# A hybrid retention and delta-rule step: the first block's triangular inverse moved from VectorE and DMA to TensorE, and small scalings moved to ScalarE

## The chip, the cores and the metric

The kernel runs on one core of a Trainium2 chip. The metric is device time in microseconds from the start to the end of one execution; the time before is the median of three runs. A change of less than 0.3% can't be told from no change. TensorE is PE in the profile's rows, VectorE is DVE, ScalarE is ACT, GpSimd is POOL and SyncE is SP.

## The reference

One decoder layer for 2048 new tokens and for 8 short sequences of 8 tokens. Half of the heads are retention heads (`ret`), the other four are gated delta heads (`gdn`). For a delta head and a chunk of tokens the reference solves a unit lower triangular system and carries a state S:

```
kk = einsum('bhid,bhjd->bhij', ki, ki)
A = where(strict, bi[..., :, None] * kk * dmat, 0.0)
rhs = concatenate([ki * (bi * exp(cum))[..., None], vi * bi[..., None]])
sol = triangular_solve(eye + A, rhs, lower=True, unit_diagonal=True)
v_new = u - einsum('bhcd,bhde->bhce', w, S)
scores = einsum('bhid,bhjd->bhij', qi, ki) * dmat
o = einsum(qi * exp(cum), S) + einsum(scores, v_new)
S = exp(cum[-1]) * S + einsum(ki * tail, v_new)
```

q, k and v of a delta head pass through a causal convolution with four taps and a SiLU first. An output projection with two norms and an MLP (squared ReLU, width 4096) follow. All is float32; the large products are made from a high and a low part, three products for each.

## The kernel before, in words

The 2048 tokens are four blocks (b = 0 to 3) of T = 512, each of NC = 4 chunks of 128; the 64 short tokens ride with block 1. A block has three stages: the input projections of its heads (`proj`), the output projection (`out_proj`) and the MLP. The MLP of a block is merged with the projections of the next, so that from block 1 on the heads' small steps lie between large products of two kinds. Block 0 has no block before it: its heads have only its own projections beside them. Weights are split into high and low parts on their first use (ScalarE the high, GpSimd the low) and stored in memory for later blocks.

The order of TensorE's instructions is written out by the program: a planner (`Weave`) emits the main stream, and side streams (one or two heads at a time) give up the engine for a number of planned microseconds at each `yield LAT[...]`. In block 0 two delta streams run, heads 0 and 2 in one and 1 and 3 in the other. TensorE executes in this order, and an instruction whose data are late holds up all that are behind it. The tiles of heads 0 and 2 are called XX, ym, mt, kv; those of heads 1 and 3 lie in one page called bhi, and their q, k, v in blo.

`gdn_head` makes for a head: the decay matrix Dm (four operations, one for each chunk, which multiply by the upper mask U and by cc, the scale of k with beta), the products mt = (k k, k q) times Dm, then the inverse XT of the triangular matrix of each chunk, v scaled (vr), and the recurrence over the four chunks. The inverse is made in two parts. The blocks of 32 are inverted on VectorE, with moves of 16x16 blocks between partitions by 19 small DMAs for a head that GpSimd issues. Then two levels of doubling (32 and 64) on TensorE bring them to 128: transpose XT, copy it to X (ScalarE), multiply with the level's part ms of the matrix, copy to Y (ScalarE), multiply with XT, subtract from XT (VectorE).

```
px = v4(mx())
for c in range(NC):
    transpose(px[:, c], XT[:, c], P)
act(X, px, AF.Copy)
...
    matmul(py[:, c], ms[:, c], X[:, c])
act(Y, py, AF.Copy)
...
    matmul(pt[:, c], Y[:, c], XT[:, c])
tt(XT, XT, pt, ALU.subtract)
```

`conv_channel` makes the four taps of a convolution on VectorE: a product for the first tap, then three multiply-adds; there are 12 channels of 128 in each block. `act` is an operation of ScalarE, `tt`, `tsc` and `stt` are of VectorE (two tensors, tensor and scalars, two tensors and a scalar).

Of the kernel before, what the change touches and what calls it, by code (L numbers as in the profile page):

```python
# [21 lines left out]
H = 4  # L22
# [27 lines left out]
C_ER = C_VD + H  # L50
C_VDS = C_ER + H
C_ERS = C_VDS + H
C_END = C_ERS + H
C_L = C_END
C_LS = C_L + P
C_ALL = C_LS + NS
# [6 lines left out]
def const_table():  # L63
    i = np.arange(P)
    c = np.zeros((P, C_ALL), np.float64)
    c[:, C_ID:C_ID + P] = np.eye(P)
    c[:, C_U:C_U + P] = i[:, None] <= i[None, :]
    c[:, C_L:C_L + P] = i[:, None] > i[None, :]
    for n, s in enumerate(LEVELS):
        c[:, C_M + n * P:C_M + (n + 1) * P] = level_mask(i, s)  # L70
    same = i[:, None] // BB == i[None, :] // BB
    c[:, C_BD:C_BD + P] = same
    c[:, C_BS:C_BS + P] = -1.0 * (same & (i[:, None] < i[None, :]))
    j = np.arange(NS)
# [12 lines left out]
    return c.astype(np.float32)  # L87


def rope_table(nb):  # L90
# [8 lines left out]

TUNE = dict(  # L100
    first=dict(
        conv=7.29, inv=41.8, mem=7.63, pace=0.08, gate=10.83, h2=10.56, rstd=16.8, hk=1.57, put=1.7, gate2=1.82, sc=2.02, gs=9.72,
        g1=2.55, g2=2.75, g3=0.91, g4=2.06, g5=0.58, c1=1.61, c2=1.07, c3=0.99, glate=4.36, s1=7.06, s2=1.58, s3=0.83,
        s4=1.43, s5=0.98, s6=0.86, s7=1.7, r0=2.61, rs=1.89, r1=1.4, r2=2.98, r3=0.73, rlate=6.88, t1=7.35, t2=0.71,
        st=3.5, dg=1.65, n0=0.08, n1=2.49, n2=3.62, n3=1.1, f0=0.1, f1=1.8, f2=1.2),
# [97 lines left out]
def hybrid_kernel(ctx: ExitStack, tc: tile.TileContext, I, O, NB: int, SB: int):  # L203
# [48 lines left out]
    def stt(out, in0, scalar, in1, op0, op1):  # L252
        return V.scalar_tensor_tensor(out=out, in0=in0, scalar=scalar, in1=in1, op0=op0, op1=op1)  # L253

    def tt(out, a, b, op, eng=None):
        return (eng or V).tensor_tensor(out=out, in0=a, in1=b, op=op)  # L256

    def tsc(out, a, s1, s2, op0, op1=None, eng=None):
        if op1 is None:
            return (eng or V).tensor_scalar(out=out, in0=a, scalar1=s1, scalar2=None, op0=op0)  # L260
        return (eng or V).tensor_scalar(out=out, in0=a, scalar1=s1, scalar2=s2, op0=op0, op1=op1)
# [19 lines left out]
    Us = cst[:NS, C_US:C_US + NS]  # L281
    smask = [cst[:NS, C_MS + n * NS:C_MS + (n + 1) * NS] for n in range(len(SLEVELS))]
    bmask = cst[:NS, C_BM:C_BM + NSEQ]
    Lr = const.tile([P, P], F32R, name="Lr")
    Lsr = const.tile([NS, NS], F32R, name="Lsr")
    L, Ls = Lr.bitcast(F32), Lsr.bitcast(F32)
# [134 lines left out]
    class Block:  # L421
# [232 lines left out]
        def conv_channel(self, ct, pss, out, outs, raws):  # L654

            raw = page([P, NTM], "raw", bufs=2)
            V.tensor_copy(raw[:, 0:3], hist[:, ct, :])
            for (n0, n1), ps in zip(self.halves, pss):
                w = min(n1, T) - n0
                act(raw[:, 3 + n0:3 + n0 + w], ps[:, :w], AF.Copy)  # L660
                if n1 > T:
                    V.tensor_copy(raws[:, :, 3:], ps[:, T - n0:n1 - n0].rearrange("p (s l) -> p s l", s=NSEQ))
            V.tensor_copy(hist[:, ct, :], raw[:, T:T + 3])
            tsc(out, raw[:, 0:T], cw[:, ct, 0:1], None, ALU.mult)
            for j in range(1, 4):
                stt(out, raw[:, j:j + T], cw[:, ct, j:j + 1], out, ALU.mult, ALU.add)
            th = raw[:, 0:T]
            act(th, out, AF.Tanh)
            stt(out, th, 1.0, out, ALU.add, ALU.mult)
            if self.samp:  # L670
                V.tensor_copy(raws[:, :, 0:3], scv[:, ct])
                V.tensor_copy(scv[:, ct], raws[:, :, LS:LS + 3])
                y = outs.rearrange("p (s l) -> p s l", s=NSEQ)
                tsc(y, raws[:, :, 0:LS], cw[:, ct, 0:1], None, ALU.mult)
                for j in range(1, 4):
                    stt(y, raws[:, :, j:j + LS], cw[:, ct, j:j + 1], y, ALU.mult, ALU.add)
                th = junk()[:, :NS]
                act(th, outs, AF.Tanh)
                stt(outs, th, 1.0, outs, ALU.add, ALU.mult)
# [51 lines left out]
        def gdn_head(self, h):  # L731
# [48 lines left out]
            X, XT = XX[:, 0], XX[:, 1]  # L780
            Dm = X
            act(Dm.rearrange("p c i -> p (c i)"), ps, AF.Exp)
            for c in range(NC):
                stt(Dm[:, c], Dm[:, c], cc[:, c:c + 1], U, ALU.mult, ALU.mult)
            yield LAT["g1"]

            mt = get(mtp, "mt").rearrange("p (c a d) -> p c a d", c=NC, a=2)
            for cp in range(0, NC, 2):
                pm = mx().rearrange("p (c a i) -> p c a i", c=2, a=2)
                for c in (cp, cp + 1):  # L790
                    matmul(pm[:, c - cp], kq[:, 0, c * P:(c + 1) * P], kq[:, :, c * P:(c + 1) * P])
                tt(mt[:, cp:cp + 2], pm, Dm[:, cp:cp + 2].unsqueeze(2).to_broadcast([P, 2, 2, P]), ALU.mult)

            ym = quad(get(ymp, "ym"))
            Y, ms = ym[:, 0], ym[:, 1]
            nb = NC * NB16
            yf, prod = (ap.rearrange("p c d -> p (c d)") for ap in (Y, ms))
            w = NC * BB
# [53 lines left out]
            tt(XT.rearrange("p c (b i) -> p c b i", b=NB16), spread(xc), blk(bd), ALU.mult)  # L852
            tt(xo, spread(cm), blk(mask[0]), ALU.mult)
            tt(XT, XT, ms, ALU.subtract)

            pv = mx()
            for c in range(NC):
                transpose(pv[:, c * P:(c + 1) * P], vf[:, c * P:(c + 1) * P], P)
            tt(vr, v4(pv), per4(rin), ALU.mult)
            yield LAT["inv"]  # L860

            for n in range(1, len(LEVELS)):
                px = v4(mx())
                for c in range(NC):
                    transpose(px[:, c], XT[:, c], P)
                act(X, px, AF.Copy)
                tt(ms, mt[:, :, 0, :], bc4(mask[n]), ALU.mult, eng=G)
                yield LAT["g2" if n == 1 else "g5"]
                py = v4(mx())
                for c in range(NC):  # L870
                    matmul(py[:, c], ms[:, c], X[:, c])
                act(Y, py, AF.Copy)
                yield LAT["g3"]
                pt = v4(mx())
                for c in range(NC):
                    matmul(pt[:, c], Y[:, c], XT[:, c])
                tt(XT, XT, pt, ALU.subtract)
                yield LAT["g4"]
            W.signal(self.key(f"y{h}"))

            S = Sg[:, h, :]
            og = X
            so = small([P, 8], "so")
            for c in range(NC):
                kc, qc = kq[:, 0, c * P:(c + 1) * P], kq[:, 1, c * P:(c + 1) * P]
                p1 = mx()
                matmul(p1[:, :P], kc, S)
                matmul(p1[:, P:2 * P], qc, S)
                R = small([P, P], f"R{st}", bufs=1)
                stt(R, p1[:, :P], nce[:, c:c + 1], vr[:, c], ALU.mult, ALU.add)  # L890
                act(og[:, c], p1[:, P:2 * P], AF.Copy, scale=E[:, 0, h, c:c + 1])
                yield LAT["c1"]
                p2 = mx()
                matmul(p2[:, :P], XT[:, c], R)
                vn = small([P, P], f"vn{st}", bufs=1)
                act(vn, p2[:, :P], AF.Copy)
                yield LAT["c2"]
                p3 = mx()
                matmul(p3[:, P:2 * P], kt[:, c], vn)
                matmul(p3[:, :P], mt[:, c, 1, :], vn)  # L900
                stt(S, S, E[:, 2, h, c:c + 1], p3[:, P:2 * P], ALU.mult, ALU.add)
                tt(og[:, c], og[:, c], p3[:, :P], ALU.add)
                act(junk(), og[:, c], AF.Square, accum_out=so[:, c:c + 1])
                if c < NC - 1:
                    yield LAT["c3"]
            if b == NB - 1:
                nc.gpsimd.dma_start(O["gdn_p"][:, h, :], S)
            W.signal(self.key(f"q{h}"), 0.0)
            stt(so[:, :NC], so[:, :NC], 1.0 / DK, eq, ALU.mult, ALU.add)
            rsqrt(so[:, :NC], so[:, :NC], NC)  # L910
            tt(og, og, per4(so[:, :NC]), ALU.mult)
            yield LAT["glate"]
            po = mx()
            for c in range(NC):
                transpose(po[:, c * P:(c + 1) * P], og[:, c], P)
            self.put_mix(H + h, po, 0, zf)

        def gdn_sample(self, h):
            sc, LAT = self.sc, self.lat
# [624 lines left out]
```

## Time and profile before

| what | value |
|---|---|
| median of 3 runs | 3052.93 us (3044.34 to 3053.2) |
| the profiled execution | 3054.3 us, its span 3052.5 us |
| TensorE busy | 2857.7 us (94%) |
| VectorE busy | 1559.1 us (51%) |
| ScalarE busy | 879.6 us (29%) |
| GpSimd busy | 861.1 us (28%) |

The span is from the first to the last instruction. A busy TensorE is not one at its peak: its granted clock has two levels, and a matmul at the lower takes twice as long. What is idle on TensorE, and what ended each idle stretch, is read from the waits.

### The profile page before, as it was taken

The page shows a single profiled execution, that of the slowest core. Times are in us where ns is not written, and L with a number is a line of the kernel's source. Part 1 is how long each engine was busy: PE and PEld are TensorE (multiplying, and loading weights), DVE is VectorE, ACT ScalarE, POOL GpSimd, SP SyncE. Part 2 cuts the span into 40 slices and gives each one's busy share as a digit, 9 for nine tenths or more (in the row PEclk, how much of TensorE's full clock was granted, in tenths as well). Part 3 has the DMA queues.
Part 4 walks back from the last instruction along what each step waited for, and adds up shares of the span by engine and source line. Part 5 has one row for each costly group of instructions (what it writes and reads, how often), then busy time and mean ns, then how long its engine had stood idle before and what let it go on. Part 6 is the DMA issues. An engine that isn't in the chain of part 4 may idle for free.

```text
span 3052.5 us, 43157 instructions
## 1 busy us (share of the span) xinstructions
PE 2857.7 (94%) x16072; PEld 2468.2 (81%) x16072; DVE 1559.1 (51%) x3282; ACT 879.6 (29%) x2365; POOL 861.1 (28%) x1040
## 2 busy tenths in 40 slices
PE   7876788998999989899999999999999999999998
PEld 6765788786877768788988989978888887888887
DVE  6968566637473652655254545265454635332113
ACT  4333332323232332332221332232222222221111
POOL 6546332526153542512020211131121212120000
PEclk9988899999999999899999999999999999999999
DMA  8545373656655556764445454675455555665554
GB/s 315 192 148 172 131 260 134 222 173 214 208 176 204 184 212 232 260 234 155 165 151 180 151 188 159 206 263 171 161 193 179 179 177 187 221 249 180 187 197 170
DMA packets 193169, 590.59 MB, mean 193 GB/s; under 512 B 28512, under 2 KB 35552, under 8 KB 192960
## 3 DMA queue, kind: packets, MB, share of 16 engines
q1 hardware_dynamic: 157520, 498.29, 47.3%
q0 software_dynamic: 34288, 87.45, 8.8%
q8 instruction: 127, 2.08, 0.3%
q10 hardware_dynamic: 1152, 2.10, 0.2%
q14 instruction: 82, 0.67, 0.1%
HBM read 443.02 MB, written 137.79 MB: 190 GB/s over the span
## 4 chain that ended last, share of the span: by engine, by line
PE 55%; DVE 4%; DMA 2%; issue 1%; POOL 1%; ACT 0%; DVEq 0%; POOLq 0%; ACTq 0%
PE mm L268 49%; PE mx L268 4%; PE mx L272 1%; DVE ym L256 1%; DVE XX L256 1%; DMA x1d<-mt 1%; DMA ym<-xf 0%; DMA ym<-ym 0%; DMA XX<-ym 0%; DVE mt L256 0%; DVE ym L253 0%; DMA xin<-in_w_down 0%; DVE raw L256 0%; DVE a L256 0%; POOL ym L848 0%
## 5 line engine op out<-in xcount | busy, mean ns | idle before, releaser
L268 PE MATMUL mm<-ahi,wpc 128*128 128x512 f32 (+2 forms) x3040 | 873.0, 363 | 4.4 <-ACT wpc L250 3.1
L268 PE MATMUL mm<-wpc,fhi 128*128 128x512 f32 x2048 | 665.5, 406 | 20.1 <-DVE a L256 7.5
L268 PEld LDWEIGHTS mm<-ahi,wpc 128*128 128x128 f32 x3040 | 545.3, 190 | 86.1 <-issue 6.6
L268 PE MATMUL mm<-alo,wpc 128*128 128x512 f32 (+2 forms) x1520 | 539.8, 355 | 0.0
L268 PEld LDWEIGHTS mm<-wpc,fhi 128*128 128x128 f32 x2048 | 384.9, 192 | 112.9 <-DVE a L256 11.5
L268 PE MATMUL mm<-bhi,wpc 128*128 128x512 f32 (+2 forms) x1536 | 425.5, 353 | 0.0
L268 PE MATMUL mm<-wpc,flo 128*128 128x512 f32 x1024 | 411.4, 402 | 12.2 <-DVE flo L256 12.2
L256 POOL TENSOR_TENSOR wpc<-xin,wpc 128x512 fp32r<-128x512 f32 (+1 forms) x208 | 276.3, 1346 | 189.2 <-ACT wpc L250 174.3
L268 PEld LDWEIGHTS mm<-alo,wpc 128*128 128x128 f32 x1520 | 290.1, 191 | 33.4 <-issue 0.5
L250 ACT ACTIVATE raw<-mm 128x512 f32<-128x512 f32 (+2 forms) x226 | 115.1, 510 | 683.1 <-PE mm L268 666.1
L268 PEld LDWEIGHTS mm<-bhi,wpc 128*128 128x128 f32 x1536 | 274.5, 190 | 32.1 <-issue 0.9
L268 PE MATMUL mm<-wpc,bhi 128*128 128x256 f32 (+1 forms) x1664 | 295.2, 283 | 1.1 <-ACT bhi L250 1.1
L256 DVE TENSOR_TENSOR a<-a,mm 128x512 f32<-128x512 f32 x224 | 152.2, 684 | 239.5 <-PE mm L268 239.0
L268 PE MATMUL mm<-blo,wpc 128*128 128x512 f32 (+2 forms) x768 | 265.6, 346 | 0.0
L256 DVE TENSOR_TENSOR flo<-raw,fhi 128x512 fp32r<-128x512 f32 (+1 forms) x166 | 103.5, 624 | 307.5 <-ACT raw L250 306.9
L268 PEld LDWEIGHTS mm<-wpc,bhi 128*128 128x128 f32 x1664 | 250.2, 188 | 2.2 <-ACT bhi L250 1.4
L268 PEld LDWEIGHTS mm<-wpc,flo 128*128 128x128 f32 x1024 | 197.2, 193 | 59.8 <-DVE flo L256 13.9
L268 PE MATMUL mm<-wpc,blo 128*128 128x256 f32 (+1 forms) x768 | 214.7, 279 | 0.2 <-DVE blo L256 0.2
L250 ACT ACTIVATE wpc<-xin 128x512 fp32r<-128x512 f32 (+1 forms) x208 | 130.0, 629 | 217.9 <-PE mm L268 131.8
L268 PEld LDWEIGHTS mm<-blo,wpc 128*128 128x128 f32 x768 | 146.5, 191 | 14.7
L268 PEld LDWEIGHTS mm<-wpc,blo 128*128 128x128 f32 x768 | 144.5, 188 | 0.4 <-DVE blo L256 0.4
L256 POOL TENSOR_TENSOR a<-a,vz 128x512 f32<-128x512 f32 x28 | 35.8, 1287 | 342.5 <-ACT mx L250 342.2
(517 smaller groups left out, 3973.9 us busy)
## 6 DMA issues: line engine op xcount, KB each, us to landing
wpc<-ws SPq DMA_DIRECT2D x612, 512.0 KB, 5.0
ws<-wpc SPq DMA_DIRECT2D x204, 512.0 KB, 5.5
xin<-in_w_up SPq DMA_DIRECT2D x64, 256.0 KB, 5.2
xin<-in_w_down SPq DMA_DIRECT2D x64, 256.0 KB, 4.9
xin<-in_x_prompt POOLq DMA_DIRECT2D x56, 256.0 KB, 4.4
xin<-in_w_ret SPq DMA_DIRECT2D x28, 256.0 KB, 4.0
wpc<-ws SPq DMA_DIRECT2D x12, 528.0 KB, 5.3
mixd<-raw POOLq DMA_DIRECT2D x24, 256.0 KB, 4.7
```

Of the source, the lines that this page charges most:

```text
L250: return A.activation(out, in_, f, **kw)
L256: return (eng or V).tensor_tensor(out=out, in0=a, in1=b, op=op)
L268: return tc.keep_in_program_order(nc.tensor.matmul(out, lhsT, rhs, start=start, stop=stop))
L272: return tc.keep_in_program_order(nc.tensor.transpose(out, in_, ident[:rows, :rows]))
```

## The change

In block 0 the inverse starts from the identity minus the blocks of level 1 and is then doubled six times on TensorE (2, 4, 8, 16, 32, 64). The part of the matrix for a level up to 8 is picked on VectorE by comparing a table `lev` (which has the level as its number) with the level; 16, 32 and 64 keep their masks on GpSimd. In blocks 1 to 3 the inverse stays as it was (its code is now the method `small_blocks`). In all blocks Dm is one product with U over the four chunks, and cc is applied to mt instead (four operations for two); vr, the scaling of the outputs og by their norm, and the first tap of each convolution are made by ScalarE. The planned time `inv` of block 0 goes from 41.8 to 5.0.

```diff
-        conv=7.29, inv=41.8, mem=7.63, ...
+        conv=7.29, inv=5.0, mem=7.63, ...
...
+    for s in (1, 2, 4, 8):
+        c[:, C_LEV:C_LEV + P] += s * level_mask(i, s)
...
-            tsc(out, raw[:, 0:T], cw[:, ct, 0:1], None, ALU.mult)
+            act(out, raw[:, 0:T], AF.Copy, scale=cw[:, ct, 0:1])
...
-            for c in range(NC):
-                stt(Dm[:, c], Dm[:, c], cc[:, c:c + 1], U, ALU.mult, ALU.mult)
+            tt(Dm, Dm, bc4(U), ALU.mult)
...
-                tt(mt[:, cp:cp + 2], pm, Dm[:, cp:cp + 2].unsqueeze(2).to_broadcast([P, 2, 2, P]), ALU.mult)
+                for c in (cp, cp + 1):
+                    stt(mt[:, c], pm[:, c - cp], cc[:, c:c + 1], Dm[:, c].unsqueeze(1).to_broadcast([P, 2, P]), ALU.mult, ALU.mult)
+            levels = LEVELS[1:]
+            if b == 0:
+                levels = (2, 4, 8) + LEVELS
+                stt(ms, bc4(lev), 1.0, mt[:, :, 0, :], ALU.is_equal, ALU.mult)
+                tt(XT, bc4(ident), ms, ALU.subtract)
+            else:
+                self.small_blocks(X, XT, Y, ms, mt)
...
-            tt(vr, v4(pv), per4(rin), ALU.mult)
+            for c in range(NC):
+                act(vr[:, c], pv[:, c * P:(c + 1) * P], AF.Copy, scale=rin[:, c:c + 1])
...
-            for n in range(1, len(LEVELS)):
+            for n, size in enumerate(levels):
...
-                tt(ms, mt[:, :, 0, :], bc4(mask[n]), ALU.mult, eng=G)
+                if size in LEVELS:
+                    tt(ms, mt[:, :, 0, :], bc4(mask[LEVELS.index(size)]), ALU.mult, eng=G)
+                else:
+                    stt(ms, bc4(lev), float(size), mt[:, :, 0, :], ALU.is_equal, ALU.mult)
...
-            tt(og, og, per4(so[:, :NC]), ALU.mult)
+            for c in range(NC):
+                act(og[:, c], og[:, c], AF.Copy, scale=so[:, c:c + 1])
```

On TensorE, in block 0, this stood behind the products of head 0 (its k and q with the 256 columns, and the transposes of v); 51 products of the projections (mm) followed before the next small step, and the first doubling came 184 rows later:

```order
L268 MATMUL mx_903<-kq_631 128x256 x2
L272 MATMUL mx_964<-cst,vz_494 128x128 x4
L268 MATMUL mm_1008<-ahi_120,wpc_984 128x512
L268 MATMUL mm_1008<-alo_121,wpc_984 128x512
L268 MATMUL mm_1008<-ahi_120,wpc_984 128x512 x2
```

Now the first doubling (transposes of XX) stands 24 products behind, and between its two multiplications (XX, ym) stand six:

```order
L271 MATMUL mx_1006<-XX_880,ym_906 128x128 x4
L271 MATMUL mm_990<-ahi_120,wpc_944 128x512
L271 MATMUL mm_990<-alo_121,wpc_944 128x512
L271 MATMUL mm_990<-ahi_120,wpc_944 128x512
L271 MATMUL mm_990<-ahi_120,wpc_950 128x512
L271 MATMUL mm_990<-alo_121,wpc_950 128x512
L271 MATMUL mm_990<-ahi_120,wpc_950 128x512
L271 MATMUL mx_1018<-XX_880,ym_906 128x128 x4
```

So the doublings moved ahead of projections that used to be done before them. Toward the end of block 0's projections TensorE had this row of small steps of heads 2, 3 and of retention head 2 (flo, fhi), with no large product between them:

```order
L272 MATMUL mx_3062<-cst,bhi_2315 128x128 x4
L268 MATMUL mx_3069<-flo_2623 128x128 x4
L268 MATMUL mx_3075<-R_634_3059,XX_2058 128x128
L268 MATMUL mx_3079<-bhi_2315 128x128 x4
L268 MATMUL mx_3085<-vn_638_3077,kv_2012 128x128
L268 MATMUL mx_3085<-vn_638_3077,mt_2083 128x128
L268 MATMUL mx_3092<-bhi_2315 128x128 x4
```

The same steps of head 2, with a doubling of head 3 (bhi), now have products of the projections between them:

```order
L271 MATMUL mx_2606<-Sg,kq_1037 128x128 x2
L275 MATMUL mx_2612<-cst,bhi_2427 128x128 x4
L271 MATMUL mm_2580<-wpc_2403,ahi_120 128x256 x2
L271 MATMUL mm_2580<-wpc_2403,alo_121 128x256
L271 MATMUL mm_2580<-wpc_2403,ahi_120 128x256 x2
L271 MATMUL mm_2580<-wpc_2403,alo_121 128x256
```

The third multiplication of head 2 by R stood in row 899 and stands in row 769, with 128 instructions of doubling ahead of it that were not there. From the start of block 1's norm on (mx<-xin,ones) the order of TensorE's 13591 instructions is the same, one for one. On VectorE the piece behind head 0's products was

```order
L253 SCALAR_TENSOR_TENSOR XX_880<-XX_880,cc_864,cst 128x128 x4
L256 TENSOR_TENSOR mt_898<-mx_899,XX_880 128x512
L256 TENSOR_TENSOR mt_898<-mx_903,XX_880 128x512
L256 TENSOR_TENSOR ym_907<-mt_898,cst 128x512
L253 SCALAR_TENSOR_TENSOR blo_753<-blo_753,mm_1008 128x512
L804 TENSOR_REDUCE ym_907<-ym_907 128x64
```

and is now (the convolution of v of head 1, blo<-raw,cw,blo, follows behind both pieces):

```order
L256 SCALAR_TENSOR_TENSOR mt_895<-mx_896,cc_864,XX_880 128x256 x2
L256 SCALAR_TENSOR_TENSOR mt_895<-mx_901,cc_864,XX_880 128x256 x2
L256 SCALAR_TENSOR_TENSOR blo_753<-raw_918,blo_753 128x512
L256 SCALAR_TENSOR_TENSOR ym_906<-cst,mt_895 128x512
L259 TENSOR_TENSOR XX_880<-cst,ym_906 128x512
L256 SCALAR_TENSOR_TENSOR blo_753<-blo_753,mm_956 128x512
L256 SCALAR_TENSOR_TENSOR ym_906<-cst,mt_895 128x512 x2
L259 TENSOR_TENSOR XX_880<-XX_880,mx_1018 128x512
```

The second of the two operations ym<-cst,mt is for level 4 and writes what level 2's multiplication reads, so that it stands in VectorE's queue behind a product of TensorE, and the convolution behind it.

## Rows read from the trace of the kernel before

**Rows 1.** The page: busy us and share, then tenths in 40 slices.
```profile
span 3052.5 us, 43157 instructions
PE 2857.7 (94%) x16072; PEld 2468.2 (81%) x16072; DVE 1559.1 (51%) x3282; ACT 879.6 (29%) x2365; POOL 861.1 (28%) x1040
...
PE   7876788998999989899999999999999999999998
PEld 6765788786877768788988989978888887888887
DVE  6968566637473652655254545265454635332113
...
PEclk9988899999999999899999999999999999999999
```

**Rows 2.** Windows: width, busy by engine (instructions), granted clock, DMA share, GB/s.
```profile
36.00:120.00 84.00, 71.62 (x344) 58.64 (x343) 69.21 (x127) 32.74 (x90) 47.46 (x44) 0.97 0.71 253
120.00:250.00 130.00, 102.24 (x557) 88.12 (x558) 98.32 (x192) 46.01 (x129) 66.41 (x75) 0.88 0.47 157
250.00:395.00 145.00, 106.52 (x673) 96.52 (x673) 99.67 (x200) 45.68 (x142) 68.31 (x85) 0.85 0.40 135
...
780.00:3053.00 2273.00, 2206.48 (x12265) 1901.44 (x12264) 1032.41 (x2162) 607.01 (x1611) 483.91 (x622) 0.99 0.56 192
```

**Rows 3.** Waits of TensorE, 36 to 395 us: total us, times, longest.
```profile
PE mx L272 <- DVE XX L256: 19.8, 3, 15.1
PE mx L272 <- DVE bhi L256: 13.2, 1, 13.2
PE mx L272 <- DVE a L256: 10.3, 2, 8.6
PE mx L272 <- DVE blo L253: 10.0, 1, 10.0
PE mx L268 <- ACT bhi L250: 8.3, 4, 2.4
PE mx L268 <- DVE Sg L253: 6.9, 5, 3.9
...
PE mm L268 <- DVE alo L256: 0.2, 1, 0.2
```

**Rows 4.** Timeline of TensorE in block 0: start, us, what.
```profile
168.78 1.12 PE L272 MATMUL mx<-cst,XX 128*128 128x128 f32 x4 [15.06 <-DVE XX L256]
...
321.73 0.60 PE L272 MATMUL mx<-cst,XX 128*128 128x128 f32 x4
322.08 0.47 PE L268 MATMUL mm<-ahi,wpc 128*128 128x512 f32 x1
...
323.11 1.13 PE L268 MATMUL mx<-XX,ym 128*128 128x128 f32 x8
323.99 0.47 PE L268 MATMUL mm<-ahi,wpc 128*128 128x512 f32 x1
...
394.74 1.02 PE L268 MATMUL mx<-xin,ones 128*128 128x512 f32 x2
```

**Rows 5.** Groups of VectorE, 0 to 395 us, shapes apart: busy, mean ns.
```profile
L253 DVE SCALAR_TENSOR_TENSOR blo<-raw,cw,blo 128x512 f32<-128x512 f32 x18 | 22.5, 1250 | 0.2
...
L256 DVE TENSOR_TENSOR bhi<-bhi,cst 128x512 f32<-128x512 f32 x8 | 9.8, 1220 | 0.7 <-DMA bhi<-bhi 0.7
...
L253 DVE SCALAR_TENSOR_TENSOR XX<-XX,cc,cst 128x128 f32<-128x128 f32 x8 | 6.2, 832 | 0.0
...
L256 DVE TENSOR_TENSOR XX<-XX,mx 128x512 f32<-128x512 f32 x4 | 2.7, 684 | 2.4 <-PE mx L268 2.4
...
L260 DVE TENSOR_SCALAR kq<-raw,cw 128x512 f32<-128x512 f32 x4 | 1.9, 479 | 0.0
...
L819 DVE TENSOR_REDUCE xf<-bhi 32x2 f32<-32x2 f32 x2 | 0.3, 142 | 0.0
```

**Rows 6.** Groups of ScalarE, 0 to 395 us, shapes apart: busy, mean ns.
```profile
L250 ACT ACTIVATE XX<-mx 128x512 f32<-128x512 f32 x6 | 3.6, 596 | 20.0 <-PE mx L272 19.9
...
L250 ACT ACTIVATE XX<-mx,E 128x128 f32<-128x128 f32 x8 | 2.9, 366 | 7.2 <-DVE R L253 7.2
```

More of the change, by code (lines that the diff above doesn't have):

```diff
@@ L52 @@
 C_ERS = C_VDS + H
-C_END = C_ERS + H
+C_LEV = C_ERS + H
+C_END = C_LEV + P
 C_L = C_END
@@ L101 @@
     first=dict(
-        conv=7.29, inv=41.8, mem=7.63, pace=0.08, gate=10.83, h2=10.56, rstd=16.8, hk=1.57, put=1.7, gate2=1.82, sc=2.02, gs=9.72,
+        conv=7.29, inv=5.0, mem=7.63, pace=0.08, gate=10.83, h2=10.56, rstd=16.8, hk=1.57, put=1.7, gate2=1.82, sc=2.02, gs=9.72,
         g1=2.55, g2=2.75, g3=0.91, g4=2.06, g5=0.58, c1=1.61, c2=1.07, c3=0.99, glate=4.36, s1=7.06, s2=1.58, s3=0.83,
@@ L283, in hybrid_kernel @@
     bmask = cst[:NS, C_BM:C_BM + NSEQ]
+    lev = cst[:, C_LEV:C_LEV + P]
     Lr = const.tile([P, P], F32R, name="Lr")
@@ new lines, in gdn_head @@
+            pv = mx()
+            for c in range(NC):
+                transpose(pv[:, c * P:(c + 1) * P], vf[:, c * P:(c + 1) * P], P)
+            for c in range(NC):
+                act(vr[:, c], pv[:, c * P:(c + 1) * P], AF.Copy, scale=rin[:, c:c + 1])
+            yield LAT["inv"]
+            for n, size in enumerate(levels):
+                px = v4(mx())
+                for c in range(NC):
+                    transpose(px[:, c], XT[:, c], P)
+                act(X, px, AF.Copy)
+                if size in LEVELS:
+                    tt(ms, mt[:, :, 0, :], bc4(mask[LEVELS.index(size)]), ALU.mult, eng=G)
+                else:
+                    stt(ms, bc4(lev), float(size), mt[:, :, 0, :], ALU.is_equal, ALU.mult)
+                yield LAT["g2" if n == 0 else "g5"]
+                py = v4(mx())
+                for c in range(NC):
+                    matmul(py[:, c], ms[:, c], X[:, c])
+                act(Y, py, AF.Copy)
+                yield LAT["g3"]
+                pt = v4(mx())
+                for c in range(NC):
+                    matmul(pt[:, c], Y[:, c], XT[:, c])
+                tt(XT, XT, pt, ALU.subtract)
+                yield LAT["g4"]
@@ new lines, in gdn_head @@
+            W.signal(self.key(f"y{h}"))
+            S = Sg[:, h, :]
+            og = X
+            so = small([P, 8], "so")
+            for c in range(NC):
+                kc, qc = kq[:, 0, c * P:(c + 1) * P], kq[:, 1, c * P:(c + 1) * P]
+                p1 = mx()
+                matmul(p1[:, :P], kc, S)
+                matmul(p1[:, P:2 * P], qc, S)
+                R = small([P, P], f"R{st}", bufs=1)
+                stt(R, p1[:, :P], nce[:, c:c + 1], vr[:, c], ALU.mult, ALU.add)
+                act(og[:, c], p1[:, P:2 * P], AF.Copy, scale=E[:, 0, h, c:c + 1])
+                yield LAT["c1"]
+                p2 = mx()
+                matmul(p2[:, :P], XT[:, c], R)
+                vn = small([P, P], f"vn{st}", bufs=1)
+                act(vn, p2[:, :P], AF.Copy)
+                yield LAT["c2"]
+                p3 = mx()
+                matmul(p3[:, P:2 * P], kt[:, c], vn)
+                matmul(p3[:, :P], mt[:, c, 1, :], vn)
+                stt(S, S, E[:, 2, h, c:c + 1], p3[:, P:2 * P], ALU.mult, ALU.add)
+                tt(og[:, c], og[:, c], p3[:, :P], ALU.add)
+                act(junk(), og[:, c], AF.Square, accum_out=so[:, c:c + 1])
+                if c < NC - 1:
+                    yield LAT["c3"]
@@ new lines, in gdn_head @@
+            if b == NB - 1:
+                nc.gpsimd.dma_start(O["gdn_p"][:, h, :], S)
+            W.signal(self.key(f"q{h}"), 0.0)
+            stt(so[:, :NC], so[:, :NC], 1.0 / DK, eq, ALU.mult, ALU.add)
+            rsqrt(so[:, :NC], so[:, :NC], NC)
+            for c in range(NC):
+                act(og[:, c], og[:, c], AF.Copy, scale=so[:, c:c + 1])
+            yield LAT["glate"]
+            po = mx()
+            for c in range(NC):
+                transpose(po[:, c * P:(c + 1) * P], og[:, c], P)
@@ L796, in gdn_head, with small_blocks @@
+            self.put_mix(H + h, po, 0, zf)
+        def small_blocks(self, X, XT, Y, ms, mt):
             nb = NC * NB16
@@ L854, in gdn_head @@
             tt(XT, XT, ms, ALU.subtract)
-            pv = mx()
-            for c in range(NC):
-                transpose(pv[:, c * P:(c + 1) * P], vf[:, c * P:(c + 1) * P], P)
-            tt(vr, v4(pv), per4(rin), ALU.mult)
-            yield LAT["inv"]
-            for n in range(1, len(LEVELS)):
[L863 to L866, printed above, removed]
-                tt(ms, mt[:, :, 0, :], bc4(mask[n]), ALU.mult, eng=G)
[L868 to L910, printed above, removed]
-            tt(og, og, per4(so[:, :NC]), ALU.mult)
[L912 to L916, printed above, removed]
```

## The prediction

> **What bounds the kernel now.** I read the page first: TensorE is busy 94% of the span and no other engine over 51% [rows 1]. The slices show where the missing 6% lies: from the sixth on TensorE's digits are eights and nines, and in slices two to five they are 8, 7, 6, 7 beside VectorE's 9, 6, 8, 5, with a granted clock of eight tenths in the last three of them [rows 1]. Those slices are block 0. The windows put numbers to it. From 780 us to the end TensorE is busy 2206 of 2273 us at 0.99 of full clock, and VectorE 45%; from 36 us (the first tiles are through) to 395 us it is busy 72, 102 and 107 us of 84, 130 and 145, with clocks of 0.97, 0.88 and 0.85, while VectorE is busy 82, 76 and 69% [rows 2]. At 394.74 us stands the product with which block 1's norm begins [rows 4]; from there on the change leaves TensorE's order as it is. So the question is at what time TensorE reaches that instruction.
>
> Block 0 loses time in two ways. First its waits: 14 kinds from 36 to 395 us, the first six and the last of which stand in the rows, 78.1 us in all; VectorE ends nearly all, for tiles of the inverse (XX, bhi) or work queued behind it (a, blo, Sg) [rows 3]. Second the clock: a granted share of 0.97, 0.88 and 0.85 means 2.5 + 15.6 + 21.8 = 39.9 us of clock gone [rows 2], of which the part that fell on work is the busy share, 280.4 of 359 us or 78%: 31 us. It falls after long waits: after 15.06 us of waiting four transposes take 1.12 us [rows 4], and with no wait ahead of them 0.60.
>
> **What is removed.** The blocks' inverse on VectorE for four heads: 148 instructions from the mask products (eight of 1220 ns) to the smallest reductions (142 ns), 87.9 us in all [rows 5], with 76 DMAs, 19 for a head, by which its data went to other partitions and back. Also the four decay operations for each head (832 ns against a single one of about 700, with U read from memory as they did), and 12 first taps of at least 479 ns each [rows 5].
>
> **What is added.** On TensorE four more levels for each of four heads. A level is four transposes, 321.73 to 322.08, 0.35 us, and twice four multiplications, 323.11 to 323.99, 0.88 us each [rows 4]: 2.11 us, times 16 is 33.8 us. The engine is in order and fully used wherever it doesn't wait, so I count all of it. On VectorE 16 comparisons with `lev`, 4 subtractions from the identity and 16 subtractions of 128x512: no row shows the comparison; the nearest are 684 ns (one operand from PSUM, no contention) and 1250 ns (two from memory, beside GpSimd) [rows 5]. I take 700 ns: 25 us, bounds 24 to 38, so VectorE keeps at least 50 us less than before. On ScalarE 32 copies of 596 ns [rows 6], 19 us, hidden since ScalarE is busy 124 of 359 us [rows 2].
>
> **The scalings.** For each head and block vr and og go from one operation of 684 ns on VectorE [rows 5] to four of 366 ns on ScalarE [rows 6], 1.46 us, 0.78 us longer; a first tap goes from 479 ns [rows 5] to about 600 ns, as the copy of the same size [rows 6]. Applying cc to mt makes four operations of two. In blocks 1 to 3 I cost all of this at a gain of 2 us: TensorE is idle there only 66.5 us in 2273 [rows 2], and VectorE gives up some 12 us in each block. What hides it is the large products that lie between the heads' steps. If that cover were gone, it would cost 0.78 us for 16 heads, twice, and 0.12 us for 48 taps, 31 us; the bounds are -5 and +31.
>
> The Trainium skill (ScalarE: Activation LUTs, Rules for kernel authors) speaks against these edits: multiplications belong on VectorE. The rows agree on the price of one, 1.46 against 0.68 us. By the rule these edits would be the 31 us above; by the waits, which name VectorE, they are nothing.
>
> **What of the waits stays.** Of 78.1 us I keep 28. The smaller wait for a (10.3 less 8.6, 1.7 us [rows 3]) lies ahead of the first delta head. The 10.0 us for blo [rows 3] is the convolution of v of head 1; it gets rid of 3 us of reductions and of a tap, but has now VectorE's comparison and subtraction of head 0 ahead of it, each of which waits for TensorE; with the first doubling, which comes too early for its XT, I take 6.5 (0 to 13). The chain has 24 levels with three hand-overs each (TensorE to ScalarE, back, and over VectorE), 72. Before it had eight levels, 24 hand-overs, and four waits at them with 8.3 us [rows 3], 0.35 us each. These fell where no large product stood between; now three to twelve stand at nearly every one, so that I take 0.2 us: 14.4 (bounds 0 and 25). 5 us for the rest. Of the clock's 31 us I keep 10, since no wait over 8 us remains (bounds 3 and 35).
>
> **The sum.** -(78.1 - 28) waits, -(31 - 10) clock, +33.8 work: -37.3 us for block 0; with -2 in the others -39. The profiled execution took 3054.3 us, 1.4 above the median of the runs: 3015, and against the median **3014 us**, 1.3% faster. With the waits at 10, the clock's cost at 3 and -5 in the other blocks it is -68 - 28 + 34 - 5 = -67, 2986; with waits of 50 and a clock cost of 25 it is -28 - 6 + 34, nothing.
>
> **Rivals.**
> *The hand-overs bound block 0 (slower).* Place: the six levels of a head, where each ScalarE copy and VectorE subtraction stands in a queue with convolutions, SiLU and weight conversion, and TensorE stops at every one. For it: ScalarE's queue stood 20 us ahead of these copies [rows 6], and now there are three times as many. Against it: 0.35 us a hand-over so far. It decides from 0.75 us: waits of 13 + 72 x 0.75 = 67 cancel the gain. At 1.1 us with a clock cost of 20: waits 92, +14 - 11 + 34 - 2 = +35, 3088 us.
> *The clock isn't given back.* More small multiplications, transposes and short stops could keep it where it is, at 0.85 to 0.88 [rows 2]. Then 31 + 4 (the added work's share) stay instead of 10: 3039 us. Against it: after 780 us the same kinds of steps run at 0.99 [rows 2]. The Trainium skill (TensorE: Matmul & The Clock Gate, Part 4: PE-mode transpose) says that transposes don't count as work for the clock; by it the 64 added ones would favour this rival, but the trace shows stretches of head steps at full clock.
> *The scalings are on the path.* ScalarE's queue delays each recurrence: +31, 3045 us. For it: the longer chain of each head. Against it: the waits.
> *The weights bound block 0 instead.* Projections that come sooner would wait for conversion or DMA; GpSimd is busy 51% and DMA 50% of this stretch on average [rows 2], and none of the six large waits is for a weight [rows 3]. 3040 us.
> *All waits go.* 2986 us, above.
> *Nothing is gained,* because as much is lost at the first doublings as was waited for: 3053 us.
>
> **Chances.** The forecast 0.58 (its own range 2995 to 3035), all waits go 0.10, the clock 0.10, the scalings 0.08, the weights 0.04, nothing 0.02, the hand-overs 0.08. Faster by over 0.3% (under 3043.8; about what a measurement of this kernel can tell from no change) are the forecast, all waits, the clock and most of the weights: 0.81. Within 0.3%: the scalings, nothing and the rest: 0.11. Slower: the hand-overs, 0.08. The range is 2986 to 3047: it leaves out the hand-overs, nothing and the tails of the rest.
>
> **What would show it.** Right: the product that begins block 1's norm at about 357 us instead of 394.74; no wait for XX, bhi, a or blo over 8 us; VectorE's busy time from 36 us to that instruction near 180 instead of 267 us; a granted clock over 0.93 in block 0; from there on the span as before within 5 us. Wrong: TensorE's waits for ACT or DVE at XX, ym and bhi over 0.7 us for each hand-over; a clock under 0.9; or the instruction early and the end not, which would be the scalings.

## The result, and the profile after

The changed kernel takes **3023.97 us** (median of 7 runs, 3019.05 to 3034.86) against 3048.24 us (7 runs) of the kernel before beside it: a ratio of 0.9923, interval 0.9904 to 0.9942, so 0.8% faster. Timed again later it gave 3025.03 us and 0.9909 (0.9894 to 0.9924). The forecast was 3014. The profiled execution took 3030.91 us, 7 above the median; that of the kernel before, 3054.3 us, lies 4 to 6 above the medians of its repeats.

The page of the changed kernel, to read beside [rows 1] (busy us, then tenths in 40 slices):

```profile
span 3029.1 us, 43658 instructions
...
PE 2879.0 (95%) x16392; PEld 2490.3 (82%) x16392; DVE 1443.0 (48%) x3074; ACT 966.2 (32%) x2573; POOL 826.9 (27%) x970
...
PE   7989889899989989899999999999999999999998
...
DVE  6655466647483642655254544265353635332113
...
PEclk9999899999999999899999999999999999999999
```

VectorE's 9 and 8 in slices two and four are gone, and TensorE's slices two to five are 9, 8, 9, 8. The windows of the changed kernel up to block 1's norm, and from there on, answer to [rows 2]:

```profile
36.00:120.00 84.00, 76.69 (x372) 62.91 (x371) 60.00 (x116) 39.43 (x104) 41.71 (x35) 0.96 0.72 258
120.00:250.00 130.00, 119.75 (x777) 102.91 (x778) 71.57 (x141) 65.90 (x176) 59.20 (x55) 1.00 0.44 150
250.00:371.47 121.47, 110.86 (x747) 100.75 (x745) 55.20 (x124) 53.58 (x158) 44.84 (x44) 0.92 0.43 154
757.00:3029.00 2272.00, 2204.52 (x12291) 1902.42 (x12291) 997.86 (x2108) 654.23 (x1730) 488.19 (x625) 0.99 0.56 193
```

TensorE's waits from 36 us to that product, the first five of 16 kinds that sum to 27.4 us, and the product itself in TensorE's timeline; they answer to [rows 3] and the last of [rows 4]:

```profile
PE mx L275 <- DVE XX L259: 5.0, 2, 4.1
PE mx L271 <- DVE Sg L256: 3.9, 3, 2.1
PE mx L275 <- DVE flo L259: 2.6, 2, 1.9
PE mx L271 <- ACT XX L253: 2.3, 5, 1.2
PE mx L271 <- DVE R L256: 1.7, 2, 1.4
```

```profile
371.47 1.02 PE L271 MATMUL mx<-xin,ones 128*128 128x512 f32 x2
```

The product that begins block 1's norm (the landmark from here on) comes at 371.47 instead of 394.74 us, 23.3 earlier; the span behind it is 2657.6 against 2657.8 us. By this view the whole gain is block 0's. The runs below show that this view alone misleads.

### The profile page after: what moved, and what is told of

It is laid out like the page before. It is cut to its first block, busy times and chain, and to the rows that moved or that the text cites. A ratio compares the mean times of both kernels' runs of the same rounds, so it can differ in the third digit from the quotient of the medians.

```text
span 3029.1 us, 43658 instructions
## 1 busy us (share of the span) xinstructions
PE 2879.0 (95%) x16392; PEld 2490.3 (82%) x16392; DVE 1443.0 (48%) x3074; ACT 966.2 (32%) x2573; POOL 826.9 (27%) x970
## 4 chain that ended last, share of the span: by engine, by line
PE 77%; DVE 11%; DMA 5%; issue 3%; POOL 2%; ACT 2%; SPq 0%; DVEq 0%; POOLq 0%; ACTq 0%
PE mm L271 66%; PE mx L271 8%; PE mx L275 2%; DVE XX L259 1%; DVE ym L259 1%; POOL wpc L259 1%; DVE raw L259 1%; DVE mt L259 1%; DMA x1d<-mt 1%; DMA xin<-in_w_out 1%; DMA wpc<-ws 0%; DVE a L259 0%; DVE flo L259 0%; DMA xin<-in_w_down 0%; DVE blo L256 0%
## 5 line engine op out<-in xcount | busy, mean ns | idle before, releaser
L271 PEld LDWEIGHTS mm<-alo,wpc 128*128 128x128 f32 x1520 | 288.8, 190 | 34.2 <-DVE alo L259 2.2
L253 ACT ACTIVATE XX<-mx 128x512 f32<-128x512 f32 x62 | 36.9, 595 | 305.0 <-PE mx L275 304.9
```

Of the source, the lines that this page charges most:

```text
L253: return A.activation(out, in_, f, **kw)
L271: return tc.keep_in_program_order(nc.tensor.matmul(out, lhsT, rhs, start=start, stop=stop))
```

## The experiments

From the two traces I held **theory A**: the gain is VectorE being rid of the blocks' inverse, and the scalings are worth nothing. Its rivals: **B**, the scalings carry a good part; **C**, they cost time on ScalarE. A table of all runs first: landmark and the span behind it are from one profiled execution each, the ratio to the kernel before is from repeats of both kernels on one chip. The two profiled executions of the change differ by 1.4 us in the landmark and by 3.0 behind it.

| kernel | landmark us | span behind it | ratio (95%) |
|---|---|---|---|
| before | 394.7 | 2657.8 | 1 |
| the change | 371.5 | 2657.6 | 0.9923 (0.9904 to 0.9942) |
| the change again | 370.1 | 2654.6 | 0.9909 (0.9894 to 0.9924) |
| doubling alone | 389.6 | 2658.1 | 1.0000 (0.9992 to 1.0009) |
| scalings alone | 381.6 | 2644.6 | 0.9937 (0.9923 to 0.9951) |
| scalings in block 0 alone | 380.1 | 2659.8 | 0.9976 (0.9967 to 0.9985) |
| change less four levels | 334.5 | 2651.2 | 0.9802 (0.9789 to 0.9815) |
| change, old planned time | 378.7 | 2651.9 | 0.9949 (0.9937 to 0.9962) |
| change, taps back | 377.8 | 2647.3 | 0.9930 (0.9917 to 0.9943) |
| change, v and outputs back | 384.9 | 2645.1 | 0.9928 (0.9914 to 0.9942) |
| change, decay back | 377.4 | 2647.5 | 0.9922 (0.9909 to 0.9936) |
| before, with filled waits | 397.5 | 2661.9 | 1.0028 (1.0017 to 1.0038) |
| head 0 doubled | 443.3 | 2648.1 | 1.0138 (1.0125 to 1.0152) |
| heads 0 and 2 doubled | 423.1 | 2645.0 | 1.0081 (1.0069 to 1.0094) |

**The two halves.** First the doubling without the scalings. TensorE's instructions come in the order of the change here, one for one, and in the run after it in the order of the kernel before:

```diff
-            act(out, raw[:, 0:T], AF.Copy, scale=cw[:, ct, 0:1])
+            tsc(out, raw[:, 0:T], cw[:, ct, 0:1], None, ALU.mult)
...
+                stt(Dm[:, c], Dm[:, c], cc[:, c:c + 1], U, ALU.mult, ALU.mult)
...
+            tt(vr, v4(pv), per4(rin), ALU.mult)
...
+            tt(og, og, per4(so[:, :NC]), ALU.mult)
```

> The doubling on TensorE in block 0 alone; the scalings of v, outputs, first taps and mt and the four decay operations stand as before. Theory A (the gain comes from VectorE's queue being rid of the blocks' inverse; the scalings are worth nothing): 22 to 24 us under the kernel before, the product that begins block 1's norm at 368 to 375 us as in the change. Theory B (the scalings carry a good part of the gain by relieving VectorE): at most 12 us under it, that product at 382 us or later. Theory C (the scalings cost time on ScalarE): 28 us or more under it.

Then the scalings without the doubling (and with the planned time of before):

```diff
-        conv=7.29, inv=5.0, mem=7.63, ...
+        conv=7.29, inv=41.8, mem=7.63, ...
...
-            if b == 0:
+            if b < 0:
```

> The scalings, the one decay mask and cc applied at mt stand as in the change; block 0 keeps the blocks' inverse on VectorE and the order of work of the kernel before. Theory A: 0 to 6 us under the kernel before, and TensorE's long waits for XX, blo, bhi and a in block 0 are there again (60 to 80 us in all from 36 us to the product that begins block 1's norm). Theory B: 12 us or more under it. Theory C: over it by 5 to 31 us.

Measured: the doubling alone 3049.47 us against 3048.67, no change; the scalings alone 3027.95, 21 us under it. **Theory A falls and B holds.** With the doubling alone TensorE still waits 41.6 us in block 0; the largest of these waits:

```profile
PE mx L275 <- DVE XX L259: 11.1, 3, 8.3
PE mx L275 <- DVE bhi L259: 5.9, 1, 5.9
PE mx L275 <- DVE flo L259: 5.6, 2, 3.7
PE mx L271 <- DVE R L256: 3.3, 2, 2.9
```

That is 36.5 us less than the 78.1 before, and 34 us of levels were added: the trade is even. With the scalings alone the long waits are there, 64.6 us in all, with XX (10.5) and blo (7.4) first; they are 13.5 us less than before, the landmark is 13 us earlier, and 13 us more come behind it. On top of the doubling, with TensorE's order unchanged, the scalings bring the landmark 18.1 us forward: the waits fall from 41.6 to 27.4 us, those for VectorE from 33.3 to 17.9. So in block 0 the scalings act mostly through what TensorE waits for from VectorE. On top of the scalings the doubling adds 0.14 to 0.28% by the two ratios, with intervals that overlap: it brings the landmark 10 to 12 us forward, and about as much is lost behind it in the profiled executions.

**What the added levels cost.** The change without the levels 2, 4, 8 and 16 in block 0:

```diff
-                levels = (2, 4, 8) + LEVELS
+                pass
```

> As the change, but block 0 leaves out the doublings of sizes 2, 4, 8 and 16: the inverse starts at 32, so the outputs of the delta heads in block 0 are not the reference's. It measures what the 16 added levels cost. If TensorE's time for them is paid in full (33.8 us), and their hand-overs nearly nothing: 34 to 40 us under the change, so 56 to 64 us under the kernel before. If half of them fills time in which TensorE would wait anyhow: some 17 us under the change, 41 under the kernel before. If the hand-overs cost 0.35 us each (48 of them, 17 us): 51 us under the change, 75 under the kernel before.

Measured: 2988.76 us, 35 to 36 under the change's two medians; landmark 36 to 37 us earlier. The levels are paid in full. The 2 or 3 us over 33.8 aren't shown to be hand-overs: this kernel also lacks the levels' work on VectorE and ScalarE, and TensorE's waits are 28.8 us in it against 27.4 in the change.

**The clock.** The kernel before, with idle products ahead of five waits:

```diff
+    def fill(out, n):
+        for _ in range(n):
+            tc.keep_in_program_order(nc.tensor.matmul(out, ident, cst[:, 0:512], start=True, stop=True))
...
+                if b == 0 and h == 0:
+                    fill(px, 15 if n == 1 else 3)
```

> The kernel before, with 49 idle products of 128x512 that read constants ahead of its five long waits in block 0 (10 ahead of the 10.0 us for blo, 15 and 3 ahead of those of 15.1 and 3.7 us for XX, 13 ahead of the 13.2 us for bhi, 8 ahead of the 8.6 us for a). Their results are overwritten, and they take less time than the wait at each place as long as the granted clock is full. So TensorE waits no less for its data, but its clock needn't fall. By the prediction's step (the low clock cost 31 us of work, nearly all of it after such waits) the product that begins block 1's norm would come 15 to 21 us earlier, and the whole 15 to 21 us under the kernel before. If most of the low clock fell inside the waits, where it costs nothing: 5 to 10 us under it. If the low clock is not due to the waits: no change, and a granted clock still at 0.9 in block 0.

Measured: 3058.72 us, 10 over; landmark 397.45. No theory foresaw a loss. It isn't the clean test that I wanted, since VectorE's instructions also came in another order. A product ran as two halves; TensorE's timeline shows the five fills, here the largest:

```profile
162.85 13.04 PE L276 MATMUL mx<-cst 128*128 128x512 f32 x30
```

and, at another place, a wait of 10.5 us for a tile of VectorE, where the kernel before waited 1.85 us:

```profile
149.26 0.79 PE L268 MATMUL mm<-wpc,ahi 128*128 128x256 f32 x2 [10.54 <-DVE fhi L253]
```

The fills take 42.9 us in all and the waits that stay 43.0, together 7.8 more than the 78.1 before, and the landmark comes 2.7 later. So the remaining work went through about 5 us quicker, with a granted clock of 0.93 instead of 0.89 from 36 us to the landmark. That speaks for 5 to 10 and against 15 to 21, without settling it; the section on the prediction counts what the low clock cost.

**Which scaling.** With A fallen I formed D (VectorE's time in block 0 counts about one for one) and E (the order of its queue counts, and parts don't add up). The change was run again beside three kernels that each put one group of edits back; TensorE's order is the same in all four:

> The changed kernel itself, timed and profiled once more beside the next three. The runs so far gave: the doubling alone, no change (1.0000); the scalings alone, 0.9937; both, 0.9923. Theory A (the gain is VectorE being rid of the blocks' inverse, the scalings worth nothing) has fallen. Theory D in its place: in block 0 VectorE's queue sets the end; the doubling frees it of 60 us but costs TensorE 34, so alone it only trades one bound for another, and the 20 us that the scalings take from VectorE there are worth about as much in time; in blocks 1 to 3 they are worth some us too. Then: 0.992 again, the product that begins block 1's norm at 370 to 374 us, and the rest of the span 2640 to 2658 us. Theory E: the gain is a matter of the order in which VectorE's instructions happen to come, which every edit shifts, and parts don't add up.

```diff
-            act(out, raw[:, 0:T], AF.Copy, scale=cw[:, ct, 0:1])
+            tsc(out, raw[:, 0:T], cw[:, ct, 0:1], None, ALU.mult)
```

> The change with the first taps back on VectorE. Theory D: VectorE gets 6.8 us back in block 0 and up to 6 us more where the next taps wait for its shared path, so 6 to 11 us over the change, of which 5 to 9 before the product that begins block 1's norm. Theory E: anything between -5 and +15, and no relation to those numbers. If the taps on ScalarE are worth nothing: within 3 us of the change.

```diff
-                act(vr[:, c], pv[:, c * P:(c + 1) * P], AF.Copy, scale=rin[:, c:c + 1])
+            tt(vr, v4(pv), per4(rin), ALU.mult)
...
-                act(og[:, c], og[:, c], AF.Copy, scale=so[:, c:c + 1])
+            tt(og, og, per4(so[:, :NC]), ALU.mult)
```

> The change with the scalings of v and of the outputs back on VectorE. In the run with the doubling alone they took VectorE 12.5 us in block 0 (two output scalings 2992 ns each, two 1848). Theory D: 9 to 13 us over the change, most of it before the product that begins block 1's norm. If, as the prediction had it, they only move work: within 3 us. If ScalarE's longer way (1.46 against 0.68 us) counts: 3 us or more under the change.

```diff
-            tt(Dm, Dm, bc4(U), ALU.mult)
+                stt(Dm[:, c], Dm[:, c], cc[:, c:c + 1], U, ALU.mult, ALU.mult)
```

> The change with four decay operations for each head, and cc in them, as before. They and mt took VectorE 13.6 us in block 0 with the doubling alone, and take 9.4 in the change. Theory D: 3 to 5 us over the change. Theory E: any sign. In blocks 1 to 3 little, since the four operations and the two of mt take there about what the one and the four of mt take.

Measured medians: the change 3025.03, taps back 3029.32, v and outputs back 3029.78, decay back 3027.53 us: 4.3, 4.8 and 2.5 over it. None of these is clear of the change: its first ratio, 0.9923 (0.9904 to 0.9942), covers the middle of all three. The landmarks, of one execution each, move more, by 7.7, 14.8 and 7.3 us. D's sizes don't come out: from 36 us to the landmark VectorE is busy 193.5, 192.7 and 185.7 us against 186.8 in the change, so with the decay back 1.1 less, and the landmark still comes 7.3 us later. So VectorE's busy time alone doesn't set it; that it is which of its instructions stands ahead of one that TensorE waits for is my reading. It leans to E; no single group is shown to carry the gain.

**Where the scalings act.** The scalings alone, and those only in block 0:

```diff
-            act(out, raw[:, 0:T], AF.Copy, scale=cw[:, ct, 0:1])
+            if self.b == 0:
+                act(out, raw[:, 0:T], AF.Copy, scale=cw[:, ct, 0:1])
+            else:
+                tsc(out, raw[:, 0:T], cw[:, ct, 0:1], None, ALU.mult)
```

> All scalings and the one decay mask in block 0 alone; the blocks' inverse everywhere as before, and blocks 1 to 3 as before. It splits the 21 us that the scalings alone gave. By the profiled execution of that run, 13 us came before the product that begins block 1's norm (381.6 instead of 394.7 us) and 13 after it. If so: 11 to 15 us under the kernel before here, with that product at 380 to 384 us and the rest of the span as before (2655 to 2660 us). If the rest were only what block 0's order leaves behind it: 20 us or more under it. If nothing of the gain is block 0's: no change.

Measured: 3042.01 us, 7.6 under the kernel before and so less than the 11 to 15 expected; landmark 380.13, behind it 2659.8, both as expected. So of the 0.63% of the scalings 0.24% comes in block 0 and 0.39%, 12 us (7 to 17 by the two intervals), in blocks 1 to 3. There TensorE's largest group, the MLP's second product, shows one place. In the doubling alone and then in the scalings alone (by line and shape: busy, mean ns, idle time ahead and what ended it):

```profile
L271 PE MATMUL mm<-wpc,fhi 128*128 128x512 f32 x2048 | 663.4, 405 | 21.0 <-DVE a L259 7.8 <-POOL wpc L259 4.5 <-ACT wpc L253 3.7
```

```profile
L271 PE MATMUL mm<-wpc,fhi 128*128 128x512 f32 x2048 | 659.6, 403 | 10.4 <-POOL wpc L259 3.8 <-DVE a L259 3.4 <-ACT wpc L253 3.0
```

The idle time ahead of it halves, 21.0 to 10.4 us, and the products run 2 ns quicker on the mean. But this one group shows more than the whole: behind the landmark TensorE's waits of all kinds sum to 91.0 us in the first kernel and 83.8 in the second, VectorE's part to 57.6 and 55.0, and TensorE is busy 2558.2 and 2552.2 us. So about half of the 13.5 us between them is not waiting at all, and little of it is waiting for VectorE. How the scalings act in blocks 1 to 3 stays open.

**Order, and fewer heads.** The change with the planned time of before:

```diff
-        conv=7.29, inv=5.0, mem=7.63, ...
+        conv=7.29, inv=41.8, mem=7.63, ...
```

> The change with the planned time of the inverse in block 0 as before (41.8 instead of 5.0 us): TensorE takes up the first doubling later, behind other products, and the chain of 24 levels ends later. If the order of TensorE carries part of the gain: 8 to 20 us over the change, with waits at the end of block 0, where the last heads' levels have nothing beside them. If the order doesn't matter: within 3 us of it.

Measured: 3034.38 us, 0.9949 against 0.9909: 8 to 12 us over the change by its two measurements, the landmark 7 to 9 us later. The order of TensorE carries a third of the gain or more, and the doubling in the old order is not shown to be better than none (0.9937). Last, two kernels with the scalings but the doubling for one or two heads:

```diff
+            double = b == 0 and h == 0
...
-            yield LAT["inv"]
+            yield LAT["inv"] if double or b else 41.8
```

> All scalings as in the change, but only the first delta head of block 0 has its whole inverse by doubling; heads 1 to 3 keep the blocks' inverse and its planned time. TensorE gets 8.4 us of added levels instead of 33.8, and VectorE is rid of a quarter of the blocks' inverse, 22 us, ahead of the longest wait (10.5 us for XX in the run of the scalings alone). If VectorE's queue sets block 0's end up to the point where TensorE is full: that product at 365 to 372 us, and 25 to 33 us under the kernel before, 0 to 9 under the change. If all four heads must leave VectorE before it helps: 376 to 382 us, and 20 us under the kernel before, as with the scalings alone.

> As the run before it, with heads 0 and 2 of block 0 doubled: 16.9 us of added levels, 44 us off VectorE. If VectorE's queue sets the end: that product at 362 to 372 us and 24 to 36 us under the kernel before. If every added level is paid in full and nothing comes back: 4 to 8 us over the run with head 0 alone.

Measured: 3092.07 and 3073.6 us. These don't test what they were to: the planner counts in nanoseconds, so that 41.8 planned no time at all for the blocks' inverse, and TensorE stood before it. The first kernel's waits up to the landmark:

```profile
PE mx L275 <- DVE bhi L259: 61.6, 2, 31.1
PE mx L275 <- DVE XX L259: 38.3, 2, 34.2
```

Three waits of 31.1, 34.2 and 30.6 us stand one for each head left on VectorE. This is what the blocks' inverse takes when TensorE has been put right behind it, and it shows again that the plan decides. Whether fewer doubled heads with the right plan would beat the change was not tried.

## Why the prediction was right, and where it failed

The time fell inside the range, and that is luck in part: one term of the sum was too large, another was missing, and the half that was to give the gain gives nothing alone.

**What bounds the kernel** held: TensorE, and in block 0 what it waits for from VectorE [rows 3]. The landmark, forecast at about 357 us, came at 371.47. **The added work**, +33.8: the instructions up to the landmark, times their spacing where nothing is waited for (0.231 us for 512 columns of a large product, 0.119 for 256, 0.111 for a small one of 128, a quarter of a multiplication, 0.0875 for a transpose), give 247.7 us before and 281.9 after, +34.2, and the run without the levels gives 35 to 36 us. **The waits**, 78.1 to 28: 27.4. The hand-overs, priced at 0.2 us, lie within that; the first rival has no ground: TensorE's waits for ACT or DVE at XX, ym and bhi sum to 9.9 us, 0.14 for each of 72, and the largest wait for XX is 4.1 us. VectorE's busy time up to the landmark, forecast near 180, is 186.8 us. The granted clock there is 0.96, over the 0.93 asked for and up from 0.89, with 64 more transposes, so the rival of the clock falls too.

**The step that failed is the clock, -(31 - 10).** The prediction took the 39.9 us of clock gone as spread evenly over the stretch and put TensorE's busy share, 78%, of it on work: 31 us. It can be counted: in windows of 1 us from 36 us to the landmark, the share of the clock that is missing, times TensorE's busy time in the window. The kernel before lost 41.0 us of clock, 22.4 on work and 18.6 while TensorE was idle; the changed kernel lost 13.7, 10.4 of them on work. So what stays was right, 10, but there were 22.4 us to win from and not 31: the term is -12.0 instead of -21. In idle time, where it costs nothing, a quarter of the clock was missing, on work 8%. Windows of the kernel before in three of the long waits and behind them, with the granted clock third from the end:

```profile
153.70:168.70 15.00, 0.03 (x1) 0.00 (x0) 14.31 (x25) 0.63 (x1) 5.82 (x9) 0.66 0.64 220
168.70:175.00 6.30, 6.22 (x25) 5.26 (x26) 1.56 (x5) 2.35 (x4) 5.81 (x8) 0.72 0.18 32
251.00:264.70 13.70, 0.65 (x6) 0.45 (x4) 12.60 (x23) 0.63 (x1) 8.84 (x11) 0.62 0.58 192
264.70:268.00 3.30, 3.20 (x16) 3.20 (x17) 2.52 (x5) 0.76 (x3) 1.30 (x3) 0.53 0.03 8
294.00:302.80 8.80, 0.17 (x2) 0.00 (x0) 8.72 (x9) 0.04 (x1) 8.02 (x9) 0.76 0.58 199
302.80:306.00 3.20, 3.18 (x15) 3.19 (x16) 1.21 (x8) 0.60 (x1) 1.00 (x2) 0.50 1.00 301
```

The waits hold 5.1 + 5.0 + 2.1 us of lost clock with TensorE idle; the stretches behind them lost 1.7 + 1.5 + 1.6 us on work. Behind the first two the clock is then full again, behind the third it is 0.72 for 5 us more. And the changed kernel, whose clock is 0.99 from 36 to 334 us, loses 7.7 of its 10.4 us behind that, where short waits follow one another at the end of block 0:

```profile
334.00:340.00 6.00, 3.59 (x16) 3.00 (x17) 4.18 (x9) 2.10 (x6) 0.58 (x2) 0.66 0.55 173
340.00:350.00 10.00, 7.45 (x32) 6.56 (x31) 4.62 (x8) 5.60 (x16) 8.89 (x7) 0.52 0.73 258
```

The other part of the miss is a term that the prediction didn't have. From 36 us to the landmark it took 358.7 us and takes 335.5: waits -50.7, work +34.2, clock -12.0, and +5.3 of busy time that neither the spacings nor the clock hold. That rest is 9 to 11 us in the kernels without the added levels (before, the scalings alone, the change less four levels) and 15 to 16 in those with them (the change, the doubling alone). So the added levels take nearer 39 us of TensorE than 33.8 (the run without them is only 35 to 36 us quicker, since its waits are 1.4 us longer and it loses 1.9 us more to the clock), and block 0 gave -23.3 instead of -37.3. What makes up the 5 us isn't shown.

**The scalings' part was wrong, though the sum hides it.** The prediction gave all of block 0's gain to the inverse and -2 to the other blocks. The doubling alone is worth nothing (1.0000): its own waits of -36.5 only pay for its +34. The scalings alone are worth 21 us, 12 of them in blocks 1 to 3, against bounds of -5 and +31 for all blocks outside block 0. (The rival of the scalings adds its 31 to a sum that already holds the -2; it should read 3047 us.) ScalarE's prices were about right (390 ns instead of 366 for a quarter of an output, 720 instead of 600 for a tap). The error was to price the edits by the time of single instructions and by TensorE's idle time, 66.5 us in 2273: in block 0 they took 15 us off the waits for VectorE, and in blocks 1 to 3 their gain shows in TensorE's busy time as much as in its waits. The rule of the Trainium skill that multiplications belong on VectorE (ScalarE: Activation LUTs, Rules for kernel authors) agrees with the price of one, and the runs decide against it here: with the scalings on ScalarE, and the decay edit, the kernel takes 3027.95 instead of 3048.67 us.

**Why "the same from the landmark on" came true all the same.** In the change, -12 from the scalings should stand behind the landmark, and 0 to -3 does in its two profiled executions. Kernels with all or two of the three groups of edits and a later landmark, at 377 to 385 us, have 2645 to 2648 us behind it. In the change, block 1 begins with longer waits than in those. Its windows there, with the DMA share and GB/s last:

```profile
401.00:411.00 10.00, 10.00 (x87) 10.00 (x86) 5.52 (x19) 4.53 (x18) 5.19 (x10) 1.00 0.99 356
411.00:421.00 10.00, 6.33 (x32) 6.13 (x31) 3.90 (x10) 0.57 (x3) 2.43 (x5) 0.67 1.02 412
```

and, in the change run again, the waits of 355 to 432 us begin with

```profile
PE mm L271 <- DMA wpc<-ws: 2.9, 1, 2.9
PE mm L271 <- DVE mt L259: 2.8, 1, 2.8
```

A stored weight comes late while the DMA engines are full, and the clock falls behind it: the rival of the weights, not in block 0 but behind it. Full DMA engines alone don't make the wait: in the scalings alone their share is 0.91 to 1.03 over the same stretch, and the wait for a stored weight 0.2 us. The kernel with v and outputs back reaches its landmark 14.8 us later and ends only 5.3 us later. In the 62 us behind the landmark, waits and clock lost on work are 9.0 us in the change run again and 4.8 to 7.7 in those four kernels, so this place explains 1 to 4 of the 10 us given back. It was read, not tested, and two kernels say that being early alone isn't the cause: the one with the old planned time (landmark 378.7) has 2651.9 us behind it, the one less four levels (334.5) 2651.2. Nor is it the same in each execution: the two profiled ones took 3030.91 and 3026.47 us, both above their medians, and four others of the same kernel 3018.51 to 3019.29. With the same landmark these would have 2646 to 2647 us behind it, like the other kernels; no trace of one was kept. What takes the scalings' gain back there stays open. That the two cancelled in the profiled executions, and so made the forecast's last sign come true, is luck.

## What to carry to other kernels

Run each half of a change alone before believing the trace's account of the whole: here the half with the large removal was worth nothing alone, the small scalings nearly all. Where the engine that bounds the kernel runs in order and is full, as TensorE here, added work is paid in full (35 to 36 us for 33.8 counted), so a removal elsewhere must first earn that; and the plan that sets its order is part of the price (8 to 12 us here). Count a low clock window by window, against the time in which the engine works: the mean share made 31 us of 22.4.

## What the runs showed of the hardware

The same VectorE instruction, the scaling of a 128x512 output by its norm, took 681 ns on the mean for two of the heads in the kernel before and 1.79 and 4.19 us in the doubling alone (count, busy us, mean ns):

```profile
L256 DVE TENSOR_TENSOR bhi<-bhi,so 128x512 f32<-128x512 f32 x2 | 1.4, 681 | 1.1 <-POOL so L256 1.1
```

```profile
L259 DVE TENSOR_TENSOR bhi<-bhi,so 128x512 f32<-128x512 f32 x2 | 6.0, 2992 | 1.2 <-POOL so L259 1.1
```

During the longest, GpSimd was busy without a break. VectorE's and GpSimd's timelines of the doubling alone:

```profile
363.42 4.19 DVE L259 TENSOR_TENSOR bhi<-bhi,so 128x512 f32<-128x512 f32 x1
...
363.36 0.60 POOL L537 DMA_DIRECT2D xin<-in_xpT  x1
363.99 1.27 POOL L259 TENSOR_TENSOR wpc<-xin,wpc 128x512 fp32r<-128x512 f32 x1
365.19 0.57 POOL L537 DMA_DIRECT2D xin<-in_xpT  x1
365.78 1.27 POOL L259 TENSOR_TENSOR wpc<-xin,wpc 128x512 fp32r<-128x512 f32 x1
```

So a scaling that took 0.68 us in one kernel held its queue six times as long in another. The Trainium skill (SBUF — State Buffer, SBUF: two separate sides) says that VectorE, in an operation with two inputs from SBUF, and GpSimd take one pair of ports in turn, each for a whole instruction. The trace agrees in kind: the row above lies over two of GpSimd's products; but one of these takes 1.27 us, so a single turn doesn't make the 3.5 us that it is longer. No run separated GpSimd's part in it.
